# Adding every second ahead block of U from rows already in SBUF, with three row buffers and two high-part buffers

## The chip, the cores and the metric

The kernel runs on one NeuronCore of one Trainium2 chip. The metric is the device time of one execution in microseconds (us); the median over runs is compared. TensorE (PE) multiplies, VectorE (DVE) and ScalarE (ACT) do elementwise work, GpSimd (POOL) issues gathers and adding DMAs, SyncE (SP) issues the plain loads and stores. 16 DMA engines move the data.

## The reference, cut to what matters

A decoder layer over 512 tokens of width 1024, in float32: two kinds of attention, an output projection, and then PEER, a feed-forward part over 16384 single-neuron experts. The change touches PEER alone:

```python
def peer_ffn(h, w_q, keys1, keys2, u, v):          # per chunk of 128 tokens
    q = (hc @ w_q).reshape(-1, PEER_HEADS, PEER_KEY_DIM)
    s1 = einsum('chd,nd->chn', q[..., :half], k1)   # 128 keys of each side
    s2 = einsum('chd,nd->chn', q[..., half:], k2)
    v1, i1 = top_k(s1, 16); v2, i2 = top_k(s2, 16)
    best_s, best_pos = top_k(all sums v1 + v2, 16)  # 16 experts for each of 8 heads
    g = softmax(best_s)
    act = gelu(einsum('cd,chkd->chk', hc, u[expert]))
    return einsum('chk,chkd->cd', g * act, v[expert])
```

## The kernel before, in words

Three of the four token tiles (384 tokens) do PEER densely: for all 16384 experts, in 128 blocks of 128, PE forms U·h (`p_u`), ACT takes its gelu (`a`), a gate matrix with zeros for the experts that were not chosen is multiplied in, and PE adds V (`acc`). The fourth tile gathers the rows that it needs with indirect DMAs (`gu`, `gv`), four buffers for them, and DVE forms the dot products (L926).

To keep float32 precision, each product is three matmuls: high·high, high·low, low·high (`mm3`, L148 to L150). A block b of U comes as 128 rows of 1024 numbers (`u`, 512 KB). ACT copies it to the high part `uhi` (L881, rounded). The low part `ulo` is the difference of the row and its high part. It is made in one of three ways: by DVE (L886), by POOL (L886), or by ACT and a DMA: ACT writes the negated high part into `ulo` (L883), and a DMA that POOL issues adds the rows of U on top, read from DRAM a second time (L884). 48 of the blocks go the last way (b = 4 to 51, table `UDMA`); b = 0 and 52 go by POOL, the rest by DVE. The third matmul of a block, L150, is the first that needs the low part.

Four stages matter here. Up to some 430 us come attention and projections. In the **ahead stage**, from about 433 us, the first 56 blocks of U are multiplied "ahead" while the router works: for each tile j = 0, 1, 2, DVE finds the chosen experts (`route`, `choose`), `spread` (L794 to L814) turns them into columns through the PE transposes `tp_s`, `hot` writes one-hot tiles `oh` (L823, L826; two buffers), PE multiplies them to gates (`p_g`, L842), ACT stores them to `st` (L845) and SP sends them to `g_d` in DRAM. Each of the eight groups of a tile (`tg`) has two U blocks beside it. The results of the first 22 blocks are spilled to DRAM (`a_d`). Then, from about 774 us, the **V loop** runs over 128 blocks of V, with the other 72 blocks of U between them, and a short tail ends it.

A tile scheduler sets the order of each engine's instructions from the program's order and priorities; U blocks have a high priority (`UPRI`). Each engine then runs its list in order, and a waiting instruction holds up what is behind it. Tiles of one tag share buffers in turn: with n buffers, the n-th next tile waits until the first one is no longer used. Before, `u` has two buffers, `uhi` three and `ulo` three.

Of the kernel before, what the change touches and what calls it, by code (L numbers as in the profile page):

```python
# [9 lines left out]
F32 = mybir.dt.float32  # L10
F32R = mybir.dt.float32r
# [5 lines left out]
ALU = mybir.AluOpType  # L17
# [4 lines left out]
P = 128  # L22
D = 1024
KC = D // P
# [29 lines left out]
XAT = (0, 1)  # L54
UPRI = 1000
PACE = 1.02
UPOOL = tuple(range(0, 56, 4))
LAST = 4
UDMA = tuple(range(4, 52))
VRB = 3  # L60
ARB = 3
RATE = (0.2, 2.75, 1.1)
# [13 lines left out]
def hybrid_layer(ctx: ExitStack, tc, x, pos, wada, wada_n, cols, w_small, w_in_a, w_in_b, wuk, wuv,  # L76
                 w_out, w_pq, keys, ut, un, pv, gfin, cst, out):
    nc = tc.nc

    def opened(stack, name, **kw):  # L80
        if "space" not in kw:
            kw["reuse_waits"] = "tile"
        return stack.enter_context(tc.tile_pool(name=name, bufs=1, **kw))
# [63 lines left out]
    def mm3(o, ahi, alo, bhi, blo, start, stop, **kw):  # L147
        nc.tensor.matmul(o, ahi, bhi, start=start, stop=False, **kw)  # L148
        nc.tensor.matmul(o, ahi, blo, start=False, stop=False, **kw)  # L149
        nc.tensor.matmul(o, alo, bhi, start=False, stop=stop, **kw)  # L150
# [24 lines left out]
    def row_back(s, pl, tag, bufs):  # L175
        t = pl.tile([P, D], F32, tag=tag, name=f"gate{s}", bufs=bufs)
        nc.sync.dma_start(t, row_d[s].to_broadcast([P, D]))
        return t
# [95 lines left out]
    for half in range(2):  # L274
# [3 lines left out]
        for k in range(KC):  # L278
            a, b = eff[0][:, k:k + 1], mods[0][:, k:k + 1]
# [590 lines left out]
    up = opened(ctx, "up", side="right")  # L870
# [3 lines left out]

    def u_block(b, psum):
        with tc.high_priority(offset=UPRI):
            raw = up.tile([P, KC, P], F32, tag="raw", name=f"u{b}", bufs=2)
            nc.sync.dma_start(raw.rearrange("p k e -> p (k e)"), ut[b])
            hi = up.tile([P, KC, P], F32R, tag="hi", name=f"uhi{b}", bufs=3)
            lo = up.tile([P, KC, P], F32R, tag="lo", name=f"ulo{b}", bufs=3)  # L880
            nc.scalar.activation(hi, raw, AF.Copy)  # L881
            if b in UDMA:
                nc.scalar.activation(lo, raw, AF.Copy, scale=-1.0)  # L883
                nc.gpsimd.dma_start(lo.rearrange("p k e -> p (k e)"), ut[b], accum_op=ALU.add)  # L884
            else:
                (nc.gpsimd if b in UPOOL else nc.vector).tensor_tensor(lo, raw, hi.bitcast(F32), op=ALU.subtract)  # L886
        o = psum(f"p_u{b}")[:, :DT]
        for k in range(KC):
            mm3(o, hi[:, k], lo[:, k], h2[0][:, k], h2[1][:, k], k == 0, k == KC - 1)
        spilt = b < NSPILL  # L890
        a = up.tile([P, DT], F32, tag="as" if spilt else "a", name=f"a{b}", bufs=2 if spilt else NACT)
        nc.scalar.activation(a, o, AF.Gelu)  # L892
        if spilt:
            nc.sync.dma_start(a_d[b], a)
            a = a_d[b]
        acts.append(a)
# [3 lines left out]
    def u_ahead(n):  # L900
        for _ in range(n):
            if nu[0] < NAHEAD:
                u_block(nu[0], lambda n: one(n, ("pj", "po", "ix")[nu[0] % 3]))
                nu[0] += 1
# [76 lines left out]
    def v_load(b):  # L981
        if b % 8 == 0:
            gt = vp.tile([P, ND, P // 16, 8, 16], F32, tag="gt", name=f"gt{b}", bufs=2)
            for j in range(ND):
                nc.sync.dma_start(gt[:, j].rearrange("p g i t -> p g (i t)"),
                                  g_d[j][:, :, b:b + 8, :].rearrange("p g i t -> p g (i t)"))
            gts[0] = gt
        raw = vp.tile([P, D], F32, tag="raw", name=f"v{b}", bufs=VRB)
        nc.sync.dma_start(raw, pv[b * P:(b + 1) * P, :])
        late = b >= NK - LAST + VB  # L990
        if late:
            hi = up.tile([P, D], F32R, tag="hi", name=f"vhi{b}", bufs=3)
            lo = up.tile([P, D], F32R, tag="lo", name=f"vlo{b}", bufs=3)
        else:
            hi = vp.tile([P, D], F32R, tag="vhi", name=f"vhi{b}", bufs=VB)
            lo = vp.tile([P, D], F32R, tag="vlo", name=f"vlo{b}", bufs=VB)
        nc.scalar.activation(hi, raw, AF.Copy)  # L997
        nc.vector.tensor_tensor(lo, raw, hi.bitcast(F32), op=ALU.subtract)  # L998
        w = vp.tile([P, DT], F32, tag="w", name=f"w{b}", bufs=2)
        a = acts[b]  # L1000
        if b < NSPILL:
            a = vp.tile([P, DT], F32, tag="ar", name=f"ar{b}", bufs=ARB)
            nc.sync.dma_start(a, acts[b])
        nc.vector.tensor_tensor(w.rearrange("p (g t) -> p g t", t=16), a.rearrange("p (g t) -> p g t", t=16),
                                gts[0][:, :, :, b % 8, :].rearrange("p j g t -> p (j g) t"), op=ALU.mult)
        if late:
            wh, wl = (up.tile([P, DT], F32R, tag="a", name=f"{n_}{b}", bufs=NACT) for n_ in ("wh", "wl"))
        else:
            wh = vp.tile([P, DT], F32R, tag="wh", name=f"wh{b}", bufs=VB)
            wl = vp.tile([P, DT], F32R, tag="wl", name=f"wl{b}", bufs=VB)  # L1010
        nc.scalar.activation(wh, w, AF.Copy)  # L1011
        last[0] = nc.vector.tensor_tensor(wl, w, wh.bitcast(F32), op=ALU.subtract).ins  # L1012
        return wh, wl, hi, lo

    def v_mm(b, j, wh, wl, hi, lo, ns=(0, 1)):
        js = slice(j * P, (j + 1) * P)
        for i, (l, r) in enumerate(((wh, hi), (wh, lo), (wl, hi))):
            for n in ns:
                nc.tensor.matmul(accs[2 * j + n], l[:, js], r[:, n * 512:(n + 1) * 512], start=b == 0 and i == 0,  # L1019
                                 stop=b == NK - 1 and i == 2)  # L1020
# [26 lines left out]
    for b in range(NK):  # L1047
        ops = v_load(b)
        if b < NK - LAST:
            for j in range(ND):  # L1050
                v_mm(b, j, *ops)
        else:
            tail.append((b, ops))
        if b >= NSPILL and nu[0] < NK:
            u_block(nu[0], two)
            nu[0] += 1
        if b == NK - 24:
            gf = up.tile([P, D], F32, tag="raw", name="gf", bufs=2)
            nc.sync.dma_start(gf, gfin.to_broadcast([P, D]))
            gate2 = row_back(5, up, "raw", 2)  # L1060
        if b < len(steps):
            due += steps[b] * (2 * TOPK - sum(NGP)) * PACE / sum(steps)
            while due >= 1.0:
                next(gen, None)
                due -= 1.0
# [69 lines left out]
```

## Time and profile before

| | us |
|---|---|
| median of 3 runs | 1613.36 (1611.5 to 1625.25) |
| the profiled execution | 1609.18 |
| its span, first to last instruction | 1607.1 |
| PE busy | 1503.8 (94%) |
| DVE busy | 1230.5 (77%) |
| ACT busy | 753.6 (47%) |
| POOL busy | 538.8 (34%) |
| mean granted PE clock | 0.979 |

The profiled execution lies 4.2 us below the median. Matmuls are pipelined, so two that follow each other closely overlap in the trace: a group's busy time is longer than the time that it takes, and the distance from one start to the next is the measure.

### The profile page before, as it was taken

Reading aid. Unit: us, or ns where it says so; the run is one execution under the profiler, and the core shown is the slowest. Engines: PE = TensorE matmul, PEld = TensorE weight load, DVE = VectorE, ACT = ScalarE, POOL = GpSimd, SP = SyncE. Lnnn points to the kernel's source line nnn. Section 1 sums busy time; section 2 is a strip of 40 time slices with the busy share of each in tenths; the row PEclk is TensorE's granted clock in tenths of the full one; section 3 lists DMA queues with packets and bytes.
Section 4 is the critical chain, followed back from the end, with each engine's and each line's share of the span. In section 5 each row is a group of like instructions: output and inputs, shape, how many; then the busy total and the mean of one; then the engine's idle time right before and its main releaser. Section 6 shows DMA issues by size and latency. Waiting matters only on the chain.

```text
span 1607.1 us, 23098 instructions
## 1 busy us (share of the span) xinstructions
PE 1503.8 (94%) x8136; PEld 1319.1 (82%) x8138; DVE 1230.5 (77%) x2623; ACT 753.6 (47%) x1190; POOL 538.8 (34%) x439
## 2 busy tenths in 40 slices
PE   6888898999899888899999999999999999999997
PEld 5757687777788788789888999999999999998885
DVE  7698986856989798343567887888888888776886
ACT  4655446544268678586333333333333333333333
POOL 2323213112111222111003645554555555553420
PEclk7999899999999999999999999999999999999999
DMA  8233333513199999998987999999999999997974
GB/s 341 79 118 106 106 131 105 171 66 96 29 239 275 295 303 289 304 287 258 316 283 263 342 388 348 323 364 309 345 355 326 342 324 355 348 306 252 334 254 156
DMA packets 161733, 410.93 MB, mean 256 GB/s; under 512 B 12865, under 2 KB 69073, under 8 KB 158289
## 3 DMA queue, kind: packets, MB, share of 16 engines
q1 hardware_dynamic: 116832, 248.81, 45.6%
q0 software_dynamic: 43776, 159.40, 30.5%
q8 instruction: 64, 1.05, 0.3%
q10 hardware_dynamic: 1008, 1.24, 0.2%
q14 instruction: 53, 0.43, 0.1%
HBM read 375.71 MB, written 33.69 MB: 255 GB/s over the span
## 4 chain that ended last, share of the span: by engine, by line
PE 69%; DVE 10%; ACT 8%; DMA 7%; issue 5%; POOL 1%; DVEq 0%; POOLq 0%; ACTq 0%; SPq 0%
PE acc L1019 31%; PE p_u L150 8%; PE p_u L149 8%; PE p_u L148 8%; PE po L561 2%; DMA a_d<-a 2%; DMA ulo<-in_ut_dram 2%; ACT st L845 2%; PE p_g L842 1%; PE p_b L148 1%; PE tp L551 1%; ACT ulo L883 1%; PE pl L535 1%; PE p_b L150 1%; PE p_b L149 1%
## 5 line engine op out<-in xcount | busy, mean ns | idle before, releaser
L150 PE MATMUL p_u<-h,ulo 128*128 128x384 f32 x1024 | 349.0, 341 | 17.1 <-DMA ulo<-in_ut_dram 17.1
L148 PE MATMUL p_u<-h,uhi 128*128 128x384 f32 x1024 | 348.6, 340 | 3.0 <-ACT a L892 3.0
L149 PE MATMUL p_u<-h,uhi 128*128 128x384 f32 x1024 | 346.3, 338 | 0.0
L918 POOL DMA_INDIRECT gu<-in_un_dram,e x128 | 190.2, 1486 | 270.1 <-DVE gu L926 239.2
L881 ACT ACTIVATE uhi<-u 128x1024 fp32r<-128x1024 f32 x128 | 135.5, 1060 | 265.8 <-PE p_u L149 213.5
L918 POOL DMA_INDIRECT gv<-in_pv_dram,e x128 | 189.4, 1479 | 187.2 <-DVE acc L937 156.3
L1019 PE MATMUL acc<-vhi,wh 128*128 128x512 f32 x768 | 237.2, 389 | 0.6 <-ACT wh L1011 0.6
L1019 PE MATMUL acc<-vlo,wh 128*128 128x512 f32 x768 | 237.3, 389 | 0.0
L1019 PE MATMUL acc<-vhi,wl 128*128 128x512 f32 x768 | 237.1, 389 | 0.0
L150 PEld LDWEIGHTS p_u<-h,ulo 128*128 128x128 f32 x1024 | 193.7, 189 | 21.7 <-DMA ulo<-in_ut_dram 19.0
L1011 ACT ACTIVATE wh<-w 128x384 fp32r<-128x384 f32 x128 | 67.3, 525 | 302.8 <-issue 179.5
L148 PEld LDWEIGHTS p_u<-h,uhi 128*128 128x128 f32 x1024 | 193.8, 189 | 7.1 <-ACT a L892 4.0
L149 PEld LDWEIGHTS p_u<-h,uhi 128*128 128x128 f32 x1024 | 193.8, 189 | 2.9
L1012 DVE TENSOR_TENSOR wl<-w,wh 128x384 fp32r<-128x384 f32 x128 | 71.4, 558 | 136.6 <-ACT wh L1011 136.4
L926 DVE SCALAR_TENSOR_TENSOR gu<-gu,h2n 128x1024 f32<-128x1024 f32 x128 | 154.2, 1221 | 21.3 <-DMA gu<-in_un_dram,e 21.1
L1019 PEld LDWEIGHTS acc<-vlo,wh 128*128 128x128 f32 x768 | 144.0, 188 | 30.3 <-DVE vlo L998 0.4
L1019 PEld LDWEIGHTS acc<-vhi,wl 128*128 128x128 f32 x768 | 144.2, 188 | 30.1
L937 DVE SCALAR_TENSOR_TENSOR acc<-gv,w,acc 128x1024 f32<-128x1024 f32 x127 | 162.6, 1280 | 5.0 <-DMA gv<-in_pv_dram,e 4.9
L1019 PEld LDWEIGHTS acc<-vhi,wh 128*128 128x128 f32 x768 | 143.2, 188 | 25.4 <-ACT wh L1011 0.9
L998 DVE TENSOR_TENSOR vlo<-v,vhi 128x1024 fp32r<-128x1024 f32 x128 | 156.2, 1220 | 3.9 <-ACT vhi L997 3.8
L997 ACT ACTIVATE vhi<-v 128x1024 fp32r<-128x1024 f32 x128 | 135.5, 1058 | 10.3 <-PE acc L1019 4.3
L884 POOL DMA_DIRECT2D ulo<-in_ut_dram x48 | 42.5, 886 | 208.9 <-ACT ulo L883 202.4
(356 smaller groups left out, 2460.2 us busy)
## 6 DMA issues: line engine op xcount, KB each, us to landing
u<-in_ut_dram SPq DMA_DIRECT2D x128, 512.0 KB, 6.3
v<-in_pv_dram SPq DMA_DIRECT2D x128, 512.0 KB, 4.9
ulo<-in_ut_dram POOLq DMA_DIRECT2D x48, 512.0 KB, 8.3
g_d<-st SPq DMA_DIRECT2D x24, 1024.0 KB, 7.4
gt<-g_d SPq DMA_DIRECT2D x48, 512.0 KB, 8.5
wada<-in_wada_dram SPq DMA_DIRECT2D x32, 512.0 KB, 3.3
raw_b<-in_w_in_b_dram SPq DMA_DIRECT2D x12, 512.0 KB, 3.7
a_d<-a SPq DMA_DIRECT2D x22, 192.0 KB, 7.3
```

Source lines behind the costliest of these rows:

```text
L148: nc.tensor.matmul(o, ahi, bhi, start=start, stop=False, **kw)
L149: nc.tensor.matmul(o, ahi, blo, start=False, stop=False, **kw)
L150: nc.tensor.matmul(o, alo, bhi, start=False, stop=stop, **kw)
L881: nc.scalar.activation(hi, raw, AF.Copy)
L918: nc.gpsimd.indirect_dma_start(out=t, out_offset=None, in_=src, in_offset=bass.IndirectOffsetOnAxis(ap=e0[:, s:s + 1], axis=0))
L926: nc.vector.scalar_tensor_tensor(t, t, 1.0, h2n, op0=ALU.mult, op1=ALU.mult, accum_out=dot0[:, s:s + 1])
L937: nc.vector.scalar_tensor_tensor(acc0, t, w0[:, s:s + 1], acc0, op0=ALU.mult, op1=ALU.add)
L997: nc.scalar.activation(hi, raw, AF.Copy)
L998: nc.vector.tensor_tensor(lo, raw, hi.bitcast(F32), op=ALU.subtract)
L1011: nc.scalar.activation(wh, w, AF.Copy)
L1012: last[0] = nc.vector.tensor_tensor(wl, w, wh.bitcast(F32), op=ALU.subtract).ins
L1019: nc.tensor.matmul(accs[2 * j + n], l[:, js], r[:, n * 512:(n + 1) * 512], start=b == 0 and i == 0, stop=b == NK - 1 and i == 2)
```

## The change

For the 24 odd blocks from 5 to 51, the adding DMA reads the rows from the SBUF tile `u` in place of DRAM. The 24 even blocks from 4 to 50 lose ACT's negation and the DMA, and DVE subtracts; so it does for blocks 0 and 52, which POOL subtracted before. `u` gets three buffers, `uhi` two. Since the added line moves the lines below it by one, L886 of before is L887 of the change, and so on.

```diff
 PACE = 1.02
-UPOOL = tuple(range(0, 56, 4))
+UPOOL = ()
 LAST = 4
-UDMA = tuple(range(4, 52))
+URB = 3
+UDMA = tuple(range(5, 53, 2))
...
     def u_block(b, psum):
         with tc.high_priority(offset=UPRI):
-            raw = up.tile([P, KC, P], F32, tag="raw", name=f"u{b}", bufs=2)
+            raw = up.tile([P, KC, P], F32, tag="raw", name=f"u{b}", bufs=URB)
             nc.sync.dma_start(raw.rearrange("p k e -> p (k e)"), ut[b])
-            hi = up.tile([P, KC, P], F32R, tag="hi", name=f"uhi{b}", bufs=3)
+            hi = up.tile([P, KC, P], F32R, tag="hi", name=f"uhi{b}", bufs=2)
             lo = up.tile([P, KC, P], F32R, tag="lo", name=f"ulo{b}", bufs=3)
             nc.scalar.activation(hi, raw, AF.Copy)
             if b in UDMA:
                 nc.scalar.activation(lo, raw, AF.Copy, scale=-1.0)
-                nc.gpsimd.dma_start(lo.rearrange("p k e -> p (k e)"), ut[b], accum_op=ALU.add)
+                nc.gpsimd.dma_start(lo.rearrange("p k e -> p (k e)"), raw.rearrange("p k e -> p (k e)"), accum_op=ALU.add)
             else:
                 (nc.gpsimd if b in UPOOL else nc.vector).tensor_tensor(lo, raw, hi.bitcast(F32), op=ALU.subtract)
```

The other places (late tiles of V in tag `hi`, `gf` and `gate2` in tag `raw`) only follow the new numbers of buffers.

The scheduler's order changes with it. First ACT, late in the ahead stage, around the gates of group 3 of tile 2. Before:

```order
L881 ACTIVATE uhi46_7632<-u46_7630 128x1024
L883 ACTIVATE ulo46_7633<-u46_7630 128x1024
L892 ACTIVATE a43_7452<-p_u43_7427 128x384
L845 ACTIVATE st2_3_7466<-p_g2_3_0_0_7467 128x4x128
L845 ACTIVATE st2_3_7466<-p_g2_3_0_1_7477 128x4x128
L845 ACTIVATE st2_3_7466<-p_g2_3_1_0_7487 128x4x128
L845 ACTIVATE st2_3_7466<-p_g2_3_1_1_7497 128x4x128
L881 ACTIVATE uhi47_7666<-u47_7664 128x1024
L883 ACTIVATE ulo47_7667<-u47_7664 128x1024
L892 ACTIVATE a44_7540<-p_u44_7515 128x384
```

The change:

```order
L893 ACTIVATE a43_7432<-p_u43_7407 128x384
L846 ACTIVATE st2_3_7446<-p_g2_3_0_0_7447 128x4x128
L846 ACTIVATE st2_3_7446<-p_g2_3_0_1_7457 128x4x128
L846 ACTIVATE st2_3_7446<-p_g2_3_1_0_7467 128x4x128
L846 ACTIVATE st2_3_7446<-p_g2_3_1_1_7477 128x4x128
L882 ACTIVATE uhi46_7611<-u46_7609 128x1024
L893 ACTIVATE a44_7519<-p_u44_7494 128x384
L884 ACTIVATE ulo47_7645<-u47_7642 128x1024
L882 ACTIVATE uhi47_7644<-u47_7642 128x1024
L893 ACTIVATE a45_7553<-p_u45_7528 128x384
```

The high part of a block now stands one block later (uhi46 beside a44, before beside a43), and there is one negation for two blocks.

Second POOL's list at the `spread` of tile 2, where gathers stand among the adding DMAs. Before:

```order
L918 DMA gu7_8083<-in_un_dram,e0_3459 128x1024
L884 DMA ulo34_6879<-in_ut_dram 128x1024
L918 DMA gu8_8086<-in_un_dram,e0_3459 128x1024
L918 DMA gu9_8334<-in_un_dram,e0_3459 128x1024
L884 DMA ulo35_6913<-in_ut_dram 128x1024
L918 DMA gu10_8501<-in_un_dram,e0_3459 128x1024
L918 DMA gu11_8664<-in_un_dram,e0_3459 128x1024
L884 DMA ulo36_7001<-in_ut_dram 128x1024
L918 DMA gu12_8799<-in_un_dram,e0_3459 128x1024
L884 DMA ulo37_7035<-in_ut_dram 128x1024
```

The change:

```order
L885 DMA ulo37_7018<-u37_7015 128x1024
L919 DMA gu6_8056<-in_un_dram,e0_3459 128x1024
L919 DMA gu7_8059<-in_un_dram,e0_3459 128x1024
L919 DMA gu8_8062<-in_un_dram,e0_3459 128x1024
L919 DMA gu9_8310<-in_un_dram,e0_3459 128x1024
L885 DMA ulo39_7161<-u39_7158 128x1024
L919 DMA gu10_8477<-in_un_dram,e0_3459 128x1024
```

Before, the transfers of blocks 34 to 37 stand behind gathers; in the change those up to block 37 stand ahead of them, and 39 behind four.

Third DVE's list of the change at the same place (`f1_2` is what the transposes `tp_s` of tile 2 need, `tt2` reads them):

```order
L801 CAST f1_2_7053<-i1_2_7049 128x256
L927 SCALAR_TENSOR_TENSOR gu4_7930,dot0_3461<-gu4_7930,h2n_3456 128x1024
L927 SCALAR_TENSOR_TENSOR gu5_7933,dot0_3461<-gu5_7933,h2n_3456 128x1024
L887 TENSOR_TENSOR ulo38_7128<-u38_7125,uhi38_7127 128x1024
L927 SCALAR_TENSOR_TENSOR gu6_8056,dot0_3461<-gu6_8056,h2n_3456 128x1024
L927 SCALAR_TENSOR_TENSOR gu7_8059,dot0_3461<-gu7_8059,h2n_3456 128x1024
L927 SCALAR_TENSOR_TENSOR gu8_8062,dot0_3461<-gu8_8062,h2n_3456 128x1024
L808 SCALAR_TENSOR_TENSOR tt2_7060<-tp_s2_7055,tt2_7060 128x128
L812 TENSOR_TENSOR o16_2_7064<-tt2_7060,iota8_101 128x2048
```

Before, no subtraction of a U block stands between blocks 3 and 53 in DVE's list; now 18 (blocks 0, 4, 6, ... 36, beside the three of 1 to 3) stand ahead of `f1_2`, and block 38 right behind it. PE's order is the same there: the transposes stand between the matmuls of blocks 37 and 38, and the first gates of tile 2 behind those of 39.

## Rows read from the trace of the kernel before

**Rows 1.** The page: busy tenths in 40 slices of the span (DMA).

```profile
DMA  8233333513199999998987999999999999997974
```

**Rows 2.** Windows: stretch, length, busy PE/PEld/DVE/ACT/POOL (count), PE clock, DMA share, GB/s.

```profile
433.40:633.40 200.00, 179.62 (x1254) 167.32 (x1253) 176.35 (x746) 151.35 (x181) 41.28 (x49) 0.98 0.96 271
633.40:680.80 47.40, 39.59 (x260) 36.88 (x259) 17.43 (x31) 27.82 (x35) 12.56 (x13) 0.96 1.03 314
680.80:753.40 72.60, 68.55 (x550) 65.13 (x550) 32.03 (x46) 55.15 (x67) 11.33 (x11) 1.00 0.95 275
774.00:1400.00 626.00, 625.38 (x3115) 563.84 (x3114) 502.50 (x640) 225.22 (x309) 295.42 (x200) 1.00 0.94 332
```

**Rows 3.** PE's waits, 433.4 to 680.8 us: releaser, us in total, times, longest.

```profile
PE p_u L150 <- DMA ulo<-in_ut_dram: 17.1, 11, 3.7
PE p_g L842 <- ACT st L845: 5.3, 9, 1.5
PE p_g L842 <- DVE oh L826: 3.5, 3, 1.4
```

**Rows 4.** PE's waits, 774 to 1590 us: all of them.

```profile
PE acc L1019 <- ACT wh L1011: 0.6, 1, 0.6
```

**Rows 5.** DMA, 428 to 753 us: queues (packets, MB, share), issues (count, KB, us to landing).

```profile
q1 hardware_dynamic: 14256, 56.76, 48.2%
q0 software_dynamic: 8784, 31.99, 46.7%
ulo<-in_ut_dram POOLq DMA_DIRECT2D x48, 512.0 KB, 8.3
gu<-in_un_dram,e POOLq DMA_INDIRECT x13, 11.9
```

**Rows 6.** DMA, 900 to 1400 us, where POOL's queue holds gathers alone; whole-span landing of `gu`.

```profile
q0 software_dynamic: 25983, 94.58, 50.3%
...
gu<-in_un_dram,e POOLq DMA_INDIRECT x128, 7.1
```

**Rows 7.** Tile `ulo`, 428 to 754 us: ns min/median/max, first and last start; landing.

```profile
L883 ACT ACTIVATE ulo<-u x48: 1039/1043/1096, 445.6 to 736.1; 128x1024 fp32r<-128x1024 f32 x48
L886 DVE TENSOR_TENSOR ulo<-u,uhi x5: 1207/1222/1226, 435.2 to 751.4; 128x1024 fp32r<-128x1024 f32 x5
DMA to landing us min/median/max: 6.5/8.3/16.0
```

**Rows 8.** DVE's timeline around tile 2: start, us, operation, idle before and its releaser.

```profile
544.47 0.69 DVE L823 TENSOR_TENSOR oh<-tt,iota 128x1024 f16<-128x1024 f16 x1 [7.17 <-PE p_g L842]
633.39 0.29 DVE L800 CAST f<-i 128x256 f32<-128x256 int32 x1
675.06 1.23 DVE L811 TENSOR_TENSOR o<-tt,iota 128x2048 f16<-128x2048 f16 x1 [19.94 <-ACT tt L805]
```

**Rows 9.** PE's timeline: tile 2's transposes and first gates; two matmuls 36 apart; 24 gates.

```profile
672.19 0.38 PE L803 MATMUL tp_s<-cst_t,f 128*128 128x128 f32 x2
680.76 0.63 PE L842 MATMUL p_g<-oh,oh 128*128 128x128 f16 x8
...
743.12 0.33 PE L149 MATMUL p_u<-h,uhi 128*128 128x384 f32 x1
749.36 0.33 PE L149 MATMUL p_u<-h,uhi 128*128 128x384 f32 x1
750.24 1.55 PE L842 MATMUL p_g<-oh,oh 128*128 128x128 f16 x24
```

**Rows 10.** Groups of instructions, 433.4 to 680.8 us: count, busy us, mean ns, idle before.

```profile
L845 ACT ACTIVATE st<-p_g 128x512 f32<-128x512 f32 x64 | 60.9, 1090 | 6.3 <-PE p_g L842 6.3
L881 ACT ACTIVATE uhi<-u 128x1024 fp32r<-128x1024 f32 x40 | 42.4, 1059 | 45.5 <-PE p_u L149 25.5 <-DMA u<-in_ut_dram 10.0 <-issue 4.7
L918 POOL DMA_INDIRECT gu<-in_un_dram,e x13 | 13.9, 1070 | 19.5 <-DVE gu L926 12.9 <-DVE wk L729 3.0 <-DVE sel L783 1.5
L721 PE MATMUL p_sc<-keys_t,qT 128*128 128x256 f32 x30 | 8.2, 401 | 0.2 <-DVE tt L807 0.2
```

More of the change, by code (lines that the diff above doesn't have):

```diff
@@ L991, in v_load @@
         if late:
-            hi = up.tile([P, D], F32R, tag="hi", name=f"vhi{b}", bufs=3)
+            hi = up.tile([P, D], F32R, tag="hi", name=f"vhi{b}", bufs=2)
             lo = up.tile([P, D], F32R, tag="lo", name=f"vlo{b}", bufs=3)
@@ L1057, in hybrid_layer @@
         if b == NK - 24:
-            gf = up.tile([P, D], F32, tag="raw", name="gf", bufs=2)
+            gf = up.tile([P, D], F32, tag="raw", name="gf", bufs=URB)
             nc.sync.dma_start(gf, gfin.to_broadcast([P, D]))
-            gate2 = row_back(5, up, "raw", 2)
+            gate2 = row_back(5, up, "raw", URB)
         if b < len(steps):
```

## The prediction

> **What bounds the kernel now.** I read the page's slices first, then windows cut at the stage borders, then who ended PE's waits in each, then the DMA queues, and last DVE's and PE's lists at one place.
>
> In the V loop PE is busy for 625.4 of 626.0 us [rows 2], and all its waits there are one of 0.6 us [rows 4]. A U block that is late by some microseconds has a whole step of the loop as cover. So the loop, and everything behind 774 us, keeps its length, and the change can only move its start.
>
> In the ahead stage DMA is nearly full: shares of 0.96, 1.03 and 0.95 in three stretches [rows 2], while in the quarter of the program ahead of it DMA mostly stands at 1 to 3 tenths [rows 1]. There PE waits 17.1 us for adding DMAs, 5.3 for ACT's gate stores and 3.5 for one-hot tiles [rows 3]. DVE is the other loaded engine: 176.35 of 200 us up to 633.4 [rows 2], and only 32.0 of 72.6 in the last part of the stage. What happens at one place shows which of the two is late: DVE casts the indices of tile 2 at 633.39, but its next step waits 19.9 us for the transposes, until 675.06 [rows 8], because PE comes to them only at 672.19, and to tile 2's first gates at 680.76 [rows 9]. PE is late there, and DVE has slack.
>
> **The change part by part.**
>
> *DMA work, less.* In 428 to 753 us (325 us) POOL's queue takes 46.7%, 151.8 us, for 31.99 MB [rows 5]. 48 transfers of 0.524 MB are 25.2 MB of it, gathers the other 6.8. Gathers alone cost 50.3% of 500 us for 94.58 MB [rows 6], 2.66 us per MB, so 18.1 us here, and one adding DMA takes (151.8 − 18.1) / 48 = 2.79 us of all 16 engines. A plain transfer of that size takes 156.7 us / 56.76 MB × 0.524 = 1.45 us [rows 5]. 24 fewer save 67 us of some 308. No row shows one with its source in SBUF. The bounds are the plain 1.45 us below, and half more than now, 4.2 us, above, since a second piece is then read on the side that already reads and writes. I take 2.79, the nearest row. DMA would need 242 us in the stage (209 to 275 by the bounds): it stops being the bound in each case, and PE's 17.1 us should go.
>
> *ACT, less.* 24 negations of 1.04 us [rows 7], 25 us. ACT is not full (151 of 200 us) [rows 2]; I count nothing for it but shorter waits of others.
>
> *POOL.* The two subtractions and 24 issues go. In the list, blocks 34 to 37 no longer stand behind gathers that wait for DVE.
>
> *DVE, more.* 26 subtractions of 1.22 us [rows 7], 31.7 us. 18 of them, 22.0 us, stand ahead of the cast for tile 2, where DVE was busy 176.35 of 200 us. So the cast comes at 433.4 + 176.35 + 22.0 + idle = 631.7 + idle. Before, idle was 23.65 us. 7.2 us of it was one wait for gates behind a stalled PE [rows 8], which I let go. New waits for high parts I put at 1.5 us in all: 18 us of idle, cast at 649.7.
>
> *From the cast to the first gates of tile 2.* Here the list of the change decides. DVE: two dot products and the subtraction of block 38, 3.7 us. Gather 6 gets its buffer when dot product 2 ends, 2 us ahead of the cast, and lands 7.1 us after its issue [rows 6]: 5.1 us after the cast. Gathers 7 and 8 follow the dot products 3 and 4, so the eighth is done at some 9.6 us after the cast. Then the tables and first one-hot tiles: 0.3 + 1.2 + 1.2 us and six operations of 0.69 [rows 8], less a little overlap, 7.4 us: the first gates at cast + 17. PE agrees: block 39's transfer stands behind gather 9, is issued 3.6 us after the cast, lands 8.3 us later [rows 5] and block 39 is through at some 16. So 649.7 + 17 = 666.7, against 680.8: **14 us gained**.
>
> The Trainium skill, page "DMA: Bandwidth & Descriptors", section "Anatomy of one DMA — SWDGE (gpsimd) path", fits a transfer issued by GpSimd at 2.0 us plus its bytes over 436 GB/s; for 512 KB that is 3.2 us, an estimate of that page. This case's rows say 8.3 us for the adding ones (6.5 at least [rows 7]) and 7.1 to 11.9 for gathers, and I sum by them. By the page gather 6 would be there before its turn, and the gates would come at cast + 15, 2 us sooner; with 11.9 us [rows 5] they would come at cast + 22.
>
> *The last eight gate groups, 680.8 to 753.4.* No wait for an adding DMA is left there to win: PE is busy 68.55 of 72.6 us [rows 2]. A block takes 24 × (749.36 − 743.12) / 36 = 4.16 us, 24 gates 1.55 us [rows 9]. With two high-part buffers, the high part of an even block starts when the block two before it is through, and DVE's subtraction follows: 1.06 + 1.22 us [rows 7, 10], with a block of 4.16 us as cover. An odd block's transfer is issued some 2.6 us behind that point and lands 8.3 us later, 10.9 us, against two blocks and 32 gates, 10.4 us. On this sum it costs 0.5 us for each of six groups, 3 us, with nothing for the emptier DMA. I take zero, since the landing should shorten, and keep 3 us in the range. `u`'s third buffer covers the time for which a row is now held until the add has read it.
>
> *Sum.* 14 us off the profiled 1609.2 is 1595. That execution lies 4.2 us under the median; off the median, 1613.4 − 14 = **1599 us**.
>
> **The rivals.**
>
> *PE alone limits.* If nearly all of DVE's idle goes, PE's own work sets the gates of tile 2: 40 blocks × 4.16 = 166.4, 512 gates 33.1 [rows 9], scores and transposes 7 [rows 10], waits for stores and one-hot tiles 8.8 [rows 3]: 433.4 + 215.3 = 648.7, 32 us sooner, 1581. For it: PE is the late engine today. Against it: DVE would need to reach its cast with almost no idle. 22 to 32 us gained: 1581 to 1591, chance 0.14.
>
> *DVE takes it back.* Idle stays near 24 us or rises a little, gathers land as late as 11.9 us: cast at 656 to 662, gates at 674 to 684; 1606 to 1619, little or nothing gained. For it: DVE gets 22 us more in a stretch where it is 88% busy, and it runs in order. Chance 0.24.
>
> *High parts hold DVE, slower.* With two buffers, ACT may write a high part only when PE is through with the block two before it, and in its list the write can stand behind four gate stores of 1.09 us [rows 10]. DVE's subtraction waits for it in order, with `route` and `choose` behind. If idle stays at 23.65 and each of the 18 subtractions waits w more, the cast is at 655.4 + 18 w. From w = 0.47 us on the kernel is slower; at w = 1.5 us gates come at 699.4, and the time is 1632. For it: before, only three subtractions stood in that stretch, so no row shows such a wait. Against: the high part has a block of 4.16 us as cover, and ACT loses 25 us of work. Chance 0.12.
>
> *The transfer from SBUF is not cheaper, or dearer* changes the sum little: at 4.2 us each DMA still has 50 us to spare. It shows in block 39's place and the last groups, some 4 us. It is in the ranges.
>
> **How the numbers follow.** The forecast, 4 to 22 us gained (idle 10 to 28 us), 1591 to 1609, has 0.50; the rivals have 0.14, 0.24 and 0.12. The range of 8 in 10 takes the forecast, the PE limit and most of the third case: 1581 to 1619. A difference of 1% (16 us) is about what can be told from no change. Over 1% faster, below 1597: the PE limit and half of the forecast's better side, 0.41. Slower by over 1%, above 1629: most of the slower rival, 0.09. Within 1%: 0.50.
>
> **What would show it.** In the profile after: DMA share of 0.75 to 0.85 in the ahead stage; PE's wait for adding DMAs at L151 under 4 us; DVE over 90% busy up to the cast of tile 2, which comes at 642 to 660; the first gates of tile 2 some 17 us behind it; the last eight groups again 72 to 75 us; the V loop as long as before. Wrong would be: PE waiting at L151 for DVE by 10 us or more, a cast behind 664, or a V loop of another length.

## The result, and the profile after

The change makes the kernel faster by a little under 1%: 1602.3 us median of 20 runs, against 1615.5 us of 20 runs of the kernel before taken beside them; the ratio is 0.9911, 95% interval [0.9888, 0.9933]. The forecast was 1599 us. The two profiled executions, 1605.42 and 1609.18 us, lie only 3.8 us apart.

Two things that have nothing to do with the change move a single execution by as much. One is the granted clock. PE runs the same first 1977 matmuls in both traces, up to the first of U block 1, yet the first U matmul starts at 433.4 us in one execution and at 435.3 in the other, and in executions of the experiments below anywhere up to 446.1, with a mean granted clock in the first 434 us between 0.95 and 0.91. Over 196 runs of 14 kernels one straight line fits: 1.41 us longer for each 0.001 less of a run's mean granted clock (0.963 to 0.981). The other is the scatter around that line, 2.1 us. So below each kernel gets two numbers: the ratio, and the difference to before **at equal clock**, from that fit, with a 95% interval.

For the change this is −11.2 ± 1.1 us. It sets the 20 runs of the change against 74 runs of the kernel before that were taken with the experiments, because the clock of the 20 beside the change is not on record. In the profiled pair the clock explains little (0.979 before, 0.978 now, 1.4 us). The profiled execution of the change lies 4.9 us above the line, further than any other of its 20 runs, and that of before 1.2 us below it: mostly scatter makes 4 us out of 11. In the profiles I compare only the **stage length**, from the first U matmul to the first V matmul: 433.4 to 775.3 = 341.9 us before, 435.3 to 768.2 = 332.9 us now, 9.0 us less.

The page's DMA slices of the kernel after, which answer to [rows 1]; in the ahead stage (slices 12 to 20) most nines have become sevens and eights:

```profile
DMA  8233233522168987978877999999998999997974
```

Windows of the kernel after: stretch, length, busy PE/PEld/DVE/ACT/POOL (count), clock, DMA share, GB/s; the whole stage, its part up to DVE's cast for tile 2, the last gate groups, and the V loop [rows 2].

```profile
435.30:768.20 332.90, 307.14 (x2173) 290.14 (x2171) 258.64 (x851) 220.70 (x269) 42.16 (x47) 0.98 0.81 249
435.30:650.00 214.70, 200.92 (x1416) 189.12 (x1415) 201.87 (x773) 150.26 (x182) 27.67 (x34) 0.97 0.80 237
671.00:745.30 74.30, 68.60 (x549) 64.53 (x548) 34.99 (x49) 50.79 (x62) 4.35 (x5) 1.00 0.76 233
768.20:1393.00 624.80, 623.07 (x3099) 561.46 (x3100) 499.56 (x635) 224.36 (x307) 297.46 (x199) 1.00 0.93 331
```

The whole stage of the kernel before, and PE's waits in it (releaser, us, times, longest):

```profile
433.40:775.30 341.90, 307.69 (x2174) 288.63 (x2172) 232.47 (x827) 243.69 (x294) 65.17 (x72) 0.98 0.96 280
```

```profile
PE p_u L150 <- DMA ulo<-in_ut_dram: 17.1, 11, 3.7
PE p_g L842 <- ACT st L845: 9.3, 17, 1.5
PE p_g L842 <- DVE oh L826: 3.5, 3, 1.4
PE p_u L148 <- ACT a L892: 3.0, 3, 1.3
```

PE's waits in the stage of the kernel after [rows 3]:

```profile
PE p_u L151 <- DMA ulo<-u: 10.1, 6, 3.0
PE p_g L843 <- ACT st L846: 7.5, 11, 2.3
PE p_g L843 <- DVE oh L827: 3.5, 6, 1.0
PE acc L1020 <- ACT wh L1012: 1.7, 1, 1.7
PE p_u L149 <- ACT a L893: 1.3, 1, 1.3
```

PE does the same work in both stages, 307.7 and 307.1 us of it. What is left of the stage, 34.2 and 25.8 us, is PE's idle time. So the stage became shorter by PE's waits, 33.7 us by name before and 25.6 after (the smallest are not shown), and 7.0 of these 8.1 us are waits for adding DMAs.

DMA of the kernel after, 428 to 745 us [rows 5]:

```profile
q1 hardware_dynamic: 14348, 57.14, 53.0%
q0 software_dynamic: 5328, 19.40, 26.2%
...
ulo<-u POOLq DMA_DIRECT2D x24, 512.0 KB, 8.2
gu<-in_un_dram,e POOLq DMA_INDIRECT x13, 9.0
```

26.2% of 317 us are 83.1 us; less 18.1 us for the gathers (in e6 below, where that queue holds gathers alone, they take 5.8% of 316.4 us, 18.4 us) that is 65 us, or 2.71 us of all 16 engines for each adding DMA from SBUF, against 2.79 from DRAM. The landing is 8.2 us, before 8.3.

DVE around tile 2 in the kernel after [rows 8], and PE's transposes and gates [rows 9]:

```profile
649.97 0.29 DVE L801 CAST f<-i 128x256 f32<-128x256 int32 x1
...
656.38 1.23 DVE L887 TENSOR_TENSOR ulo<-u,uhi 128x1024 fp32r<-128x1024 f32 x1 [3.84 <-ACT uhi L882]
...
662.17 1.22 DVE L812 TENSOR_TENSOR o<-tt,iota 128x2048 f16<-128x2048 f16 x1
```

```profile
659.48 0.38 PE L804 MATMUL tp_s<-cst_t,f 128*128 128x128 f32 x2
...
667.06 0.44 PE L151 MATMUL p_u<-h,ulo 128*128 128x384 f32 x1 [2.46 <-DMA ulo<-u]
...
671.02 1.09 PE L843 MATMUL p_g<-oh,oh 128*128 128x128 f16 x16
...
744.66 0.62 PE L843 MATMUL p_g<-oh,oh 128*128 128x128 f16 x8 [0.57 <-ACT st L846]
```

The wait of 19.94 us for the transposes is gone from DVE's list, and a wait of 3.84 us for a high part has come in. PE still comes to the transposes 9.5 us behind the cast. Before the gates it waits 2.46 us for the low part of block 39 (667.06) and then works without a pause up to 671.02.

### The profile page after: what moved, and what is told of

Its sections match the earlier page's. It is cut to its first block, busy times and chain, and to the rows that moved or that the text cites. A ratio compares the mean times of both kernels' runs of the same rounds, so it can differ in the third digit from the quotient of the medians.

```text
span 1603.6 us, 23086 instructions
## 1 busy us (share of the span) xinstructions
PE 1504.2 (94%) x8136; PEld 1321.3 (82%) x8138; DVE 1257.6 (78%) x2649; ACT 732.1 (46%) x1166; POOL 518.4 (32%) x413
## 4 chain that ended last, share of the span: by engine, by line
PE 67%; DVE 12%; DMA 8%; ACT 6%; issue 5%; POOL 1%; SPq 0%; DVEq 0%; POOLq 0%; ACTq 0%
PE acc L1020 28%; PE p_u L151 9%; PE p_u L150 9%; PE p_u L149 9%; DMA ulo<-u 3%; PE po L562 2%; PE p_g L843 2%; ACT st L846 1%; PE p_b L149 1%; PE tp L552 1%; PE p_b L151 1%; PE p_b L150 1%; PE pl L536 1%; DMA wa<-in_wada_dram 1%; DVE ulo L887 1%
## 5 line engine op out<-in xcount | busy, mean ns | idle before, releaser
L151 PE MATMUL p_u<-h,ulo 128*128 128x384 f32 x1024 | 349.6, 341 | 10.2 <-DMA ulo<-u 10.1
L919 POOL DMA_INDIRECT gv<-in_pv_dram,e x128 | 195.5, 1527 | 180.4 <-DVE acc L938 153.2
L887 DVE TENSOR_TENSOR ulo<-u,uhi 128x1024 fp32r<-128x1024 f32 x104 | 126.9, 1220 | 49.3 <-ACT uhi L882 49.2
L998 ACT ACTIVATE vhi<-v 128x1024 fp32r<-128x1024 f32 x128 | 135.5, 1059 | 10.2 <-PE acc L1020 4.3
```

What stands on the lines that cost most here:

```text
L919: nc.gpsimd.indirect_dma_start(out=t, out_offset=None, in_=src, in_offset=bass.IndirectOffsetOnAxis(ap=e0[:, s:s + 1], axis=0))
```

## The experiments

Theory 1 was that of the prediction: DMA is relieved, and then DVE's list up to the cast of tile 2 sets the length of the stage. When it fell, theory 2 took its place: the stage is PE's work plus PE's waits, and an adding DMA costs time because PE waits at the end of its chain (negation, issue, 8 us of transfer). All kernels were timed beside the kernel before. Idle is stage length less PE's busy time, in one profile; for clock and scatter see above.

| kernel | adding DMAs, source; buffers of `u`, `uhi` | ratio [95%] | at equal clock, us | stage, us | PE idle |
|---|---|---|---|---|---|
| before | 48 DRAM; 2, 3 | 1 | 0 | 341.9 | 34.2 |
| after | 24 SBUF; 3, 2 | 0.9911 [0.9888, 0.9933] | −11.2 ± 1.1 | 332.9 | 25.8 |
| e1 | 48 SBUF; 3, 2 | 1.0029 [0.9998, 1.006] | +2.7 ± 1.3 | 345.1 | 37.9 |
| e2 | 24 DRAM; 2, 3 | 0.9899 [0.986, 0.9937] | −11.3 ± 1.8 | 330.6 | 25.1 |
| e3 | 24 DRAM; 3, 2 | 0.9948 [0.992, 0.9975] | −10.2 ± 1.3 | 330.6 | 25.3 |
| e4 | 48 DRAM; 3, 2 | 0.9989 [0.9959, 1.002] | −2.6 ± 1.3 | 343.2 | 35.1 |
| e5 | 24 SBUF; 2, 3 | 1.0051 [1.0019, 1.0084] | +4.4 ± 1.3 | 352.3 | 43.3 |
| e6 | none; 3, 2 | 0.9842 [0.9802, 0.9883] | −21.4 ± 1.8 | 316.4 | 15.2 |
| e7 | 23 SBUF, early; 3, 2 | 0.9961 [0.9933, 0.999] | −8.4 ± 1.3 | 331.4 | 26.4 |
| e8 | 24 SBUF, POOL subtracts; 3, 2 | 1.0121 [1.0078, 1.0164] | +11.3 ± 1.8 | 362.6 | 50.3 |
| e10 | none, 24 spare; 3, 2 | 0.9862 [0.9817, 0.9907] | −21.1 ± 1.8 | 318.7 | 17.5 |
| e11 | 12 SBUF; 3, 2 | 0.9867 [0.9821, 0.9913] | −18.4 ± 1.8 | 320.7 | 17.1 |
| e12 | none; 2, 3 | 0.9867 [0.9821, 0.9914] | −19.6 ± 1.8 | 319.0 | 17.9 |
| e13 | none, 48 spare; 3, 2 | 1.0097 [1.007, 1.0123] | +5.8 ± 1.8 | 356.5 | 43.1 |

The equal-clock column has a limit: a kernel also moves the granted clock of its own stage. That was 0.98 before, 0.99 in e6, e10 and e12, which have little idle time, and 0.97, 0.96 and 0.95 in e5, e8 and e13, which have most. PE is busy for 301 to 313 us of the stage, least where the clock is highest, though its matmuls are the same. So the column takes out part of what such a kernel does: e13 is 5.8 us slower by it and 14.6 us longer in its stage, e6 21.4 us faster and 25.5 us shorter. Signs agree between the two columns except for e4, where the difference is within scatter.

**e1: the source alone (with the new buffers), for all 48.**

```diff
-UDMA = tuple(range(5, 53, 2))
+UDMA = tuple(range(4, 52))        # and UPOOL as before
```

> The kernel before with two things of the change alone: all 48 adding DMAs read the SBUF tile, and the buffers are three for rows and two for high parts. Theory 1 (the gain comes from half of the adding DMAs going away, the source is worth nothing): 48 transfers still take about 2.7 us of all 16 engines each, the DMA share stays at 0.93 or more up to the transposes of tile 2, PE waits 13 us or more for adding DMAs, and the time is 1609 to 1620, within 5 us of before. Rival (the source is what helps, since 25 MB of DRAM reads go): DMA share under 0.88, PE's wait under 8 us, time 1595 to 1604.

PE waits 7.6 us for adding DMAs, as the rival said, but 14.9 us for gate stores; nothing is gained (median 1621.6 us), and the DMA share of the stage stays at 0.95:

```profile
PE p_g L843 <- ACT st L846: 14.9, 18, 3.3
PE p_u L151 <- DMA ulo<-u: 7.6, 8, 2.1
```

**e4: the buffers alone** is e1 with the adding DMA reading DRAM:

```diff
-... lo ..., raw.rearrange("p k e -> p (k e)"), accum_op=ALU.add)
+... lo ..., ut[b], accum_op=ALU.add)
```

> The kernel before with the buffers alone: three for rows, two for high parts; 48 adding DMAs from DRAM. Theory 1: DMA is as full as before, PE waits 13 us or more for adding DMAs, time within 5 us of before, 1610 to 1620. Rival (a third row buffer lets rows land earlier and brings the gain): PE's wait for adding DMAs under 8 us and 1598 to 1606.

PE still waits 13.6 us for adding DMAs; 2.6 ± 1.3 us at equal clock is all that the buffers gain. e1 and e4 differ in the source alone: with 48 adding DMAs the rows from SBUF are 5.3 us slower at equal clock.

```profile
PE p_u L151 <- DMA ulo<-in_ut_dram: 13.6, 9, 3.9
```

**e2: the halving alone**, source and buffers as before:

```diff
-URB = 3
+URB = 2        # uhi: 3 buffers, source ut[b]
```

> Only the halving: 24 odd blocks by the adding DMA, which still reads DRAM, all others by DVE; two buffers for rows, three for high parts as before. Theory 1 (halving alone brings the gain): cast of tile 2 at 640 to 652, first gates some 17 to 21 us behind it, time 1597 to 1605; with three high-part buffers DVE's wait for high parts is under the 17.8 us of the changed kernel. Rival (source or buffers bring it): time 1611 to 1618.

**e3: the changed kernel with the DRAM source.** The edit is that of e4 in the changed kernel.

> The changed kernel, but the 24 adding DMAs read DRAM again (buffers three and two as changed). Theory 1: an adding DMA costs 2.7 to 2.8 us of all engines from either source and there is DMA to spare, so the time is that of the changed kernel within 4 us, 1598 to 1606. Rival (the source helps): 1610 to 1617.

e2 and e3 have the whole gain. By its median e3 looks 5.6 us slower than the change; its runs had a median clock of 0.9735, those of the change 0.977, and at equal clock 1.0 us is left between them. The halving is what gains; the new source adds nothing to it. **e5: halving and source, old buffers:**

```diff
-URB = 3
+URB = 2        # uhi: 3 buffers, source the SBUF tile
```

> The changed kernel with the old buffers: two for rows, three for high parts; the 24 adding DMAs read SBUF. Theory 1: neither the source nor the buffers matter once half of the adding DMAs are gone; from the first U matmul to the first V matmul 329 to 335 us (341.9 before, 332.9 changed), time 1597 to 1604. Rival (a row held until the add has read it needs the third buffer): that stretch 337 us or more, time 1606 to 1615.

Slower than before, and 15.7 us slower at equal clock than e2, which differs in the source alone. Now each row is held until the adding DMA has read it, and with two buffers the row after the next comes late. ACT's longest wait in the stage, and PE's, in e5:

```profile
ACT uhi L882 <- DMA u<-in_ut_dram: 70.7, 16, 10.8
```

```profile
PE p_g L843 <- ACT st L846: 21.1, 13, 4.5
```

ACT stands in order at the high part of the late row, and the gate stores stand behind it. One such place, ACT and PE:

```profile
695.64 1.06 ACT L882 ACTIVATE uhi<-u 128x1024 fp32r<-128x1024 f32 x1 [10.84 <-DMA u<-in_ut_dram]
696.61 1.04 ACT L884 ACTIVATE ulo<-u 128x1024 fp32r<-128x1024 f32 x1
697.55 0.47 ACT L893 ACTIVATE a<-p_u 128x384 f32<-128x384 f32 x1
697.92 3.68 ACT L846 ACTIVATE st<-p_g 128x512 f32<-128x512 f32 x4
```

```profile
698.99 0.79 PE L843 MATMUL p_g<-oh,oh 128*128 128x128 f16 x8 [4.51 <-ACT st L846]
```

In the change SyncE's row loads wait for adding DMAs just as long in all (140.0 us, in e5 129.6), but ACT then waits for rows only 1.2 us. So the third row buffer is the price of the SBUF source: 15.6 us at equal clock between e5 and the change. The two differ in the buffers of `uhi` too; a third row buffer by itself was not run with this source.

**e6: no adding DMA at all**, DVE subtracts all 56 blocks.

```diff
-UDMA = tuple(range(5, 53, 2))
+UDMA = ()
```

> The changed kernel without any adding DMA: DVE subtracts all 56 blocks. Theory 1 (after the change DVE's list up to the cast of tile 2 sets the time): 17 more subtractions of 1.22 us, 20.8 us, stand ahead of the cast, which comes 230 to 240 us behind the first U matmul (214.7 changed); first U to first V matmul 345 to 355 us, time 1611 to 1624, although PE waits for no adding DMA. Rival (DMA and the adding transfers still set it): DMA share under 0.7, time under 1598.

The cast came where theory 1 put it, 680.1 − 445.5 = 234.6 us behind the first U matmul (with 23 more subtractions ahead of it, not 17, but shorter waits), 20 us later than in the change, and yet the stage is 16.5 us shorter and the kernel the fastest of all. The window of the stage, PE's waits, and the place of tile 2 in e6:

```profile
445.50:761.90 316.40, 301.20 (x2173) 285.85 (x2171) 284.38 (x876) 200.89 (x245) 24.20 (x23) 0.99 0.64 221
```

```profile
PE p_g L843 <- DVE oh L827: 6.1, 8, 1.6
PE p_g L843 <- ACT st L846: 4.8, 10, 1.0
PE tp_s L804 <- DVE f L801: 2.2, 1, 2.2
```

```profile
680.64 0.38 PE L804 MATMUL tp_s<-cst_t,f 128*128 128x128 f32 x2
...
689.59 1.09 PE L843 MATMUL p_g<-oh,oh 128*128 128x128 f16 x16
```

DVE is busy 284 of 316 us and PE waits for its cast just 2.2 us: the scheduler has moved the transposes of tile 2 in PE's list from behind 38 U blocks to behind 43. A late cast makes PE do U blocks first, which it has to do anyway. Theory 1 falls. Of the 16.5 us, 10.6 are idle time of PE, and its wait for adding DMAs was 10.1; the other 5.9 are busy time, at a granted clock of 0.99 for 0.98. **e7: the table that follows theory 1.**

```diff
-UDMA = tuple(range(5, 53, 2))
+UDMA = tuple(b for b in range(4, 38) if b % 3)
```

> A table that follows theory 1: ahead of the cast of tile 2, where DVE is full, two of three blocks by the adding DMA (22 of blocks 4 to 37), and behind it, where DVE idles, all by DVE. Theory 1: seven subtractions and their waits less ahead of the cast, which comes 198 to 208 us behind the first U matmul, the first gates of tile 2 at 220 to 229 (235.7 changed); DMA share up to there 0.82 to 0.9; time 1588 to 1597. Rival (DMA becomes the bound again, or PE's own work is): gates at 234 or later, time 1600 or more.

The cast came at 217.0 us, not at 203: the list has six subtractions less ahead of it, and DVE's work up to it fell by 6.4 us (201.9 to 195.5), but its waits for high parts rose from 9.6 to 15.0. The table holds 23 blocks, not 22, and PE waits 9.7 us for them, nearly as for the 24 of the change, wherever they stand. DVE's wait up to the cast, and PE's in the stage:

```profile
DVE ulo L887 <- ACT uhi L882: 15.0, 8, 4.9
```

```profile
PE p_u L151 <- DMA ulo<-u: 9.7, 4, 4.1
```

**e8: POOL subtracts the even blocks.**

```diff
-UPOOL = ()
+UPOOL = tuple(range(4, 52, 2))
```

> The changed kernel, with the 24 even blocks subtracted by POOL (2.57 us each) in place of DVE. Theory 1: DVE is relieved of 20 us and of its waits for high parts, cast of tile 2 at 185 to 198 us behind the first U matmul, first gates of tile 2 at 215 to 229, set by PE's own work, time 1582 to 1595. Rival (POOL works in order, so its subtraction waits for the high part and for gathers, and the adding DMA of the next odd block stands behind it): PE waits 15 us or more for low parts, time 1602 or more.

The rival's case. POOL's subtraction waits in order for ACT's high part, and adding DMAs and gathers stand behind it; PE then waits for low parts. POOL's longest wait in the stage, and PE's:

```profile
POOL ulo L887 <- ACT uhi L882: 165.7, 20, 18.3
```

```profile
PE p_u L151 <- DMA ulo<-u: 24.2, 10, 7.6
PE p_g L843 <- ACT st L846: 7.3, 14, 1.0
PE p_u L151 <- POOL ulo L887: 6.5, 2, 6.2
```

**e10: 24 spare adding DMAs beside e6.** They read the odd rows, and nothing reads what they add up.

```diff
+            if b in GHOST:        # range(5, 53, 2); ghost: 128 x 768, SBUF
+                nc.gpsimd.dma_start(ghost, raw...[:, :768], accum_op=ALU.add)
```

> The kernel without adding DMAs for low parts (DVE subtracts all 56 blocks), and beside it 24 adding DMAs of 384 KB from the odd row tiles into a spare tile that nothing reads. What is tested is which part of an adding DMA costs time. Theory 2 (the cost is that PE waits for a low part at the end of a chain of negation, issue and 8 us of transfer): nobody waits for these, so PE's named waits stay near 15 us, first U to first V matmul 314 to 321 us (316.4 without them), time 1591 to 1598. Rival (the load on the DMA engines costs, since rows, gathers and spills come later): three quarters of the 11 us per 24 adding DMAs come back, 324 us or more, time 1600 or more.

The DMA share rises from 0.64 to 0.81, the same as in the change, and the time stays: −21.1 against −21.4 us. So at this share neither the load of these DMAs nor their place in POOL's list costs what can be measured. What is left is the chain that PE waits for. Which of its links costs (ACT's negation, which e10 lacks too, the issue or the transfer), no run shows. The stage in e10:

```profile
435.80:754.50 318.70, 301.22 (x2174) 286.00 (x2172) 284.22 (x876) 200.90 (x245) 53.89 (x47) 0.99 0.81 250
```

**e11: twelve adding DMAs.**

```diff
-UDMA = tuple(range(5, 53, 2))
+UDMA = tuple(range(7, 53, 4))
```

> The changed kernel with 12 adding DMAs (blocks 7, 11, ... 51) in place of 24, DVE subtracts the rest. Theory 2 (each adding DMA costs about 0.45 us, since 48, 24 and 0 gave 0, -11 and -21 us at equal clock): about -16 us against before at equal granted clock, time 1596 to 1602 at a clock of 0.976, first U to first V matmul 322 to 328 us. Rival (theory 1, DVE's list ahead of the cast, or a step between 24 and none): -12 us or less, or -20 or more.

With 48, 24, 12 and none: 0, −11.2, −18.4, −21.4 us. More than the −16 of a straight line, and the stage of 320.7 us is shorter than forecast, but both lie between their neighbours; PE waits 1.8 us for twelve. So not every adding DMA costs the same, and 0.45 us each is no price. **e12: e6 with the buffers of before** (`URB = 2`, three for `uhi`).

> No adding DMA at all, and the buffers of before: two for rows, three for high parts. Theory 2 (rows are let go early when no adding DMA reads them, so the buffers do not matter): within 3 us of the same kernel with three and two, 1590 to 1597. Rival (the third row buffer is worth something by itself): 1600 or more.

The median, 1599.1 us, lies 2 us above the forecast, at a median clock of 0.9725 against 0.9765 in e6; at equal clock it is 1.8 us from e6, within their scatter. **e13: spare DMAs beside 48 blocks.**

```diff
+GHOST = tuple(range(4, 52))        # two spare tiles of 384 columns, two DMAs a block
```

> As with the 24 spare adding DMAs (DVE subtracts all 56 blocks, nothing reads what the DMAs add), but beside each of blocks 4 to 51: 384 KB of each row tile, in two transfers of 192 KB into two spare tiles. The DMA share of the stage comes near that of the kernel before, 0.9 or more. Theory 2 (what an adding DMA costs is PE's wait at the end of its chain, not its load): first U to first V matmul 315 to 323 us, time 1591 to 1600, PE's named waits under 22 us. Rival (a nearly full DMA costs time by itself, as rows and gathers land later): that stretch 328 us or more, time 1604 or more; most of the 21 us would come back.

The rival's time, but not by the rival's reason alone: the two spare tiles make each transfer wait for the one before it (POOL 197 us), the rows are held meanwhile, and the next loads wait for that. SP's longest wait, at the row load of a U block:

```profile
SPq L884 <- DMA ghost<-u: 233.2, 45, 11.1
```

This is e5's mechanism again. What a nearly full DMA (0.91 here, 0.96 before) costs by itself, without held rows, is left open.

## Why the prediction was right, and where its reasons were not

- **V loop of the same length: right.** From the first to the last V matmul of the first form 820.3 us before, 822.5 after. All that lies behind the first V matmul is 3.6 us longer in the profiled pair (831.8 and 835.4); over the profiles of all kernels it is 831 to 836 us.
- **DMA relieved: right in size, wrong in what it brings.** A share of 0.75 to 0.85 was forecast; 0.80 up to the cast and 0.76 in the last groups are shown, and 2.71 us a transfer for the 2.79 taken. But PE's wait for adding DMAs, which was to fall under 4 us, is 10.1 us for half as many. The step "it stops being the bound in each case, and PE's 17.1 us should go" failed: the landing stayed at 8.2 us in an emptier DMA, and PE's wait for each adding DMA went from 0.36 us (17.1 for 48) to 0.42 (10.1 for 24). The Trainium skill, page "DMA: Bandwidth & Descriptors", section "Anatomy of one DMA — SWDGE (gpsimd) path", gives an estimate of 3.2 us for this size. The medians of 7.2 (e1) to 8.3 us, at DMA shares of the stage from 0.80 to 0.96, stand against it.
- **DVE's cast at 649.7 us: right, in the sum.** 649.97, or 214.7 us behind the first U matmul, where 216.3 was meant. DVE's busy time was 201.9 us against 198.4 forecast, the idle time 12.8 against 18: the waits for gates (11.1 us before, 2.2 now), for ACT's index copies (8.0 and 0.2) and for scores (2.3 and none) went nearly altogether, and the new one for high parts took 9.6 us instead of 1.5. That these errors cancel is luck.
- **17 us from the cast to the gates: mis-sized, 21.0.** The terms for the tables and one-hot tiles (0.3 + 1.2 + 1.2 + 6 × 0.69) add up to 6.8 us, not 7.4. But it was the other path, which the prediction gave 16 us, that set the gates. The high part of block 38 waited, as it has two buffers, until PE was through with block 36, which stood behind gates that waited for a store; DVE's subtraction waited 3.84 us for it. Block 39's adding DMA was issued at 657.98, 8.0 us behind the cast for 3.6 forecast, and took 9.05. In e2, with three high-part buffers, it is 18.4 us (656.15 to 674.59).
- **Last eight groups unchanged: right**, 73.6 us from the first gates to the last start, before 72.0.
- **14 us gained: 11.2 ± 1.1 at equal clock, 9.0 in the profiled stage**; 1602.3 us for 1599. The rest of the 13.2 us between the medians is not resolved; the clock of the 20 runs of before that they rest on is not on record. The forecast started from a median of 1613.4 (3 runs), 2.1 us under that of the 20.
- **The reason behind the sum was the wrong one.** It followed the cast of tile 2, and so DVE. But PE comes to the transposes of tile 2 38.8 us behind the cast before and 9.5 us behind it now, so the cast held up PE in neither. e6 has the cast 20 us later and a stage 16.5 us shorter; e7 takes six subtractions away and gains nothing. The cast moves the place at which PE turns to tile 2, not the amount of PE's work. The sum came out near partly by luck: the cast was timed rightly but did not matter, and the gates behind it were set by PE and the adding DMA of block 39. The case "PE alone limits" (22 to 32 us) is what e6 nearly is, with 21.4 us at equal clock.
- **High parts hold DVE, slower: its wait came, its price did not.** 9.6 us in 10 waits up to the cast, and DVE's other waits vanished in turn. Nor is it the two buffers: with three (e2) the same waits up to 700 us add up to 17.0 us, with two (after) to 17.8.

## What to carry to other kernels

Where one engine is nearly full, take the length of a stage as its work plus its named waits, and price a change by the waits it removes there; the time at which another engine reaches some milestone says little when a scheduler can put other work ahead of it. An adding DMA that saves an elementwise pass puts its landing, some 8 us here, into the chain of the engine that waits for it; 1.22 us on a busy but uncritical engine was cheaper, and no adding DMA at all (e6, ratio 0.9842 [0.9802, 0.9883]) beat both kernels. A transfer that reads a buffer holds it until it lands: count buffers by landings, and compare runs at the same granted clock before a difference under 1% is put down to an edit, with an eye on the clock that the edit itself moves.

## What the runs showed of the hardware

- The clock granted in the same first 434 us differs from one execution to the next: mean 0.94 and first U matmul at 433.4 us (before), 0.92 and 443.8 (e1), 0.91 and 446.1 (e12).
- The mean clock granted in the ahead stage went with PE's idle time there: 0.99 with 15.2 us idle (e6), 0.98 with 34.2 (before), 0.97 with 43.3 (e5), 0.96 with 50.3 (e8), 0.95 with 43.1 (e13).
- An adding DMA of 512 KB costs about the same from SBUF as from DRAM, 2.71 (after) and 2.79 us (before) of all 16 engines, an estimate from the queues' shares, and lands in 7.2 to 8.3 us (medians of before, after and e1 to e4) at DMA shares of the stage from 0.80 to 0.96.
- DVE's subtraction took 1.222 us in the median in e6, and just so in e10 beside 24 adding DMAs that read and write SBUF.
